# Final-norm rows and decode rows in the weight pool's slots: a hybrid decoder step on one NeuronCore

## The chip, the cores and the metric

The kernel runs on one core of a Trainium2 chip. The metric is the device time of one execution in microseconds. The core has five engines with queues of their own: PE (TensorE, matrix products), DVE (VectorE), ACT (ScalarE), POOL (GpSimd) and SP (SyncE, which here only issues DMA transfers). An engine takes its instructions strictly in the order of its queue, and an instruction that waits holds all behind it.

## The reference

One layer of a decoder trunk, for 2048 prompt rows and 8 decode rows of width 1024. Token mixing comes first (three head groups behind one input projection), then the channel mixing, and a last norm closes the trunk:

```python
mix = jnp.concatenate([y_a, y_b, y_c], axis=-1) @ w_out
x = x + gate1 * mix
hf = _rmsnorm(x, g_norm2) * (1 + scale2) + shift2
a = jax.nn.relu(hf @ w_ff1)              # hidden width 4096
x = x + gate2 * ((a * a) @ w_ff2)
...
y_prompt = _rmsnorm(xp, g_final)         # x * rsqrt(mean(x*x) + EPS) * g
y_sample = _rmsnorm(xs, g_final)
```

The change lies in the last two lines and touches nothing ahead of the product with `w_ff2`.

## The kernel before

**The second product.** `(a*a) @ w_ff2` is done in 8 passes (`NB`) over the hidden width, each with two units of 256 hidden rows (`KB = 2`). In a pass, 8 blocks follow each other, `(gi, j)` with `gi` 0 or 1 and `j` 0 to 3; a block makes two tiles of 128 rows by 1024. It uses a scheme of seven products in place of eight, each with three matmuls per unit (high and low parts), so 42 matmuls of 128x512 per block (`block`, L1805). The first four products use the first half of a block's left operands (`ai0`), the last three use the second half (`ai1`). The results lie in four PSUM banks of a block, x, y, v and z, of six there are, and DVE adds each to a sum in SBUF (`acc` for the two row tiles, `accu` for a shared term; L1396). PE can use a bank again only after DVE has drained it. In the last pass POOL and DVE then add the shared term to the row tiles.

**Operands.** The left operands of a block come by DMA from scratch memory while the block before runs (`a_load`, L1777 and L1779). For `gi = 1` one of the two units is stored unsplit, so ACT casts it (L1780) and DVE makes the low part (L1399). The right operands of a pass (tiles `wo`) are made once per pass from rows of `w_ff2` (tiles `raw2`, tag `raw` of the weight pool `wp`). Their places alternate: in every other pass, the one before the last among them, two of each unit's lie in `wp` under the tags `whi` and `wlo`; in the last pass seven of the fourteen lie in the pool `r2` under the tag `o`, and fill its 7 buffers.

**The end.** When a block of the last pass is done, its two tiles are put on a list, and `final` is called for four tiles after blocks 2, 4 and 6 and for two tiles after blocks 7 and 8. `final` squares and sums each row (ACT, L1821), multiplies half of each tile by the gain `gf` (POOL, L1832), finds the reciprocal root by a chain of small DVE operations (`row_rstd`, L188 and L119 to L124, tiles `sq`, `nr_y`, `nr_a`), scales one half on ACT (L1839) and the other on DVE (L1841), and stores each half (L1843). `samples_out` does the same for the 8 decode rows, in tiles `gs` (gate), `accs` (sum) and `xr` (residual).

**What sets the order.** The program is written by a scheduler that models each engine and puts every instruction into its engine's queue at the place where the model has it ready. A tile in a reused buffer waits for the last reader of what lay there before. SP's DMAs go through one queue; besides its data, each waits for the eighth DMA ahead of it to land.

Blocks of the last pass are called block 1 to block 8 below. Their row tiles carry these numbers in the listings: 17763 and 17765 (block 1), 17780 and 17782 (2), 17850 and 17852 (3), 17925 and 17927 (4), 17999 and 18001 (5), 18110 and 18112 (6), 18189 and 18191 (7), 18263 and 18265 (8).

Of the kernel before, what the change touches and what calls it, by code (L numbers as in the profile page):

```python
# [9 lines left out]
F32 = mybir.dt.float32  # L10
# [7 lines left out]
P = 128  # L18
D = 1024
# [30 lines left out]
R2 = 7  # L50
# [12 lines left out]
def hybrid_trunk(  # L63
# [16 lines left out]
    wp = ctx.enter_context(tc.tile_pool(name="wp", bufs=2))  # L80
# [110 lines left out]
    def load_rows(src, n, xt=None):  # L191
        if xt is None:
            xt = xpool.tile([P, D], F32, tag="x", name="xt")
        nc.sync.dma_start(out=xt[:n], in_=src)
        return xt
# [1179 lines left out]
    with ExitStack() as ph2:  # L1375
# [19 lines left out]
        def add(eng, out, in0, in1):  # L1395
            eng.tensor_tensor(out=out, in0=in0, in1=in1, op=ALU.add)  # L1396
# [268 lines left out]
        def w2_load(p, pool=None):  # L1665
            raws = []
            for i in range(2):
                raw = (pool or wp).tile([P, D], F32, tag="x" if pool else "raw", name="raw2")
                nc.sync.dma_start(out=raw, in_=w_ff2[(2 * p + i) * P:(2 * p + i + 1) * P, :])
                raws.append(raw)  # L1670
            Q.tensor_copy(out=a32[:, p % 2, :, 0:NS], in_=a_s[:, 2 * p:2 * p + 2, :])
            return raws
# [93 lines left out]
        r2 = ph2.enter_context(tc.tile_pool(name="r2", bufs=1))  # L1766
# [4 lines left out]
        def a_load(gi, j, p):  # L1771

            es = [ai.tile([P, n_, 2, P], F32R, tag=f"i{p % 2}{h}", name=f"ai{h}", bufs=2) for h, n_ in enumerate((4, 3))]
            for e, o in zip(es, (slice(0, 4), slice(4, 7))):
                e32 = e.bitcast(F32)
                if early(gi, p):
                    nc.sync.dma_start(out=e32.rearrange("p o a t -> p o (a t)"), in_=a_scr[gi][p][:, j, o])  # L1777
                else:
                    nc.sync.dma_start(out=e32[:, :, 1, :], in_=a_scr[gi][p][:, j, o])  # L1779
                    A.copy(out=e[:, :, 0, :], in_=e32[:, :, 1, :])  # L1780
                    sub(V, e[:, :, 1, :], e32[:, :, 1, :], e[:, :, 0, :])
            return es
# [3 lines left out]
        def acc_load(gi, j):  # L1786
            rows = []
            for th in range(2):
                t = 8 * gi + 4 * th + j
                r = ac.tile([P, D], F32, tag=f"r{t}", name=f"acc{t}")  # L1790
                load_rows(x1_scr[t * P:(t + 1) * P, :], P, r)
                rows.append(r)
            acc[gi, j] = rows, ac.tile([P, 512], F32, tag=f"u{gi}{j}", name=f"accu{gi}{j}")
# [29 lines left out]
        def final(tiles):  # L1823

            v = sm.tile([P, len(tiles), 2], F32, tag=f"nv{len(tiles)}", name="fv")
            if tiles[0][1] < P:
                V.memset(v, 1.0)
            for i, (x, m, _) in enumerate(tiles):
                for hf, s in enumerate(halves):
                    square_sum(x[:m, s], v[:m, i, hf:hf + 1])  # L1830
                    if hf:
                        Q.tensor_tensor(out=x[:m, s], in0=x[:m, s], in1=gf[:m, s], op=ALU.mult)  # L1832
            sq = sm.tile([P, len(tiles)], F32, tag=f"sq{len(tiles)}", name="sq")
            add(V, sq, v[:, :, 0], v[:, :, 1])
            r = row_rstd(sq, P, len(tiles), f"nr{len(tiles)}")
            for i, (x, m, dst) in enumerate(tiles):
                for hf, s in enumerate(halves):
                    if hf:
                        A.activation(out=x[:m, s], in_=x[:m, s], func=AF.Copy, scale=r[:m, i:i + 1])  # L1839
                    else:  # L1840
                        V.scalar_tensor_tensor(out=x[:m, s], in0=x[:m, s], scalar=r[:m, i:i + 1], in1=gf[:m, s],  # L1841
                                               op0=ALU.mult, op1=ALU.mult)
                    nc.sync.dma_start(out=dst[:, s], in_=x[:m, s])  # L1843

        def samples_out():
            gs, accs, xr = (r2.tile([P, D], F32, tag="o", name=n, bufs=R2) for n in ("gs", "accs", "xr"))
            nc.sync.dma_start(out=gs[0:NS].rearrange("j (k p) -> j k p", k=KT),
                              in_=g2_scr[:, 0:NS, :].rearrange("k j p -> j k p"))
            for j in range(4):
                nc.sync.dma_start(out=accs[0:NS, 256 * j:256 * j + 256], in_=chunks[32 * j:32 * j + NS])  # L1850
            load_rows(x1_scr[T:T + NS, :], NS, xr)
            Q.tensor_tensor(out=accs[:NS], in0=accs[:NS], in1=gs[:NS], op=ALU.mult)
            add(V, accs[:NS], accs[:NS], xr[:NS])
            final([(accs, NS, y_sample.rearrange("b t d -> (b t) d"))])
# [7 lines left out]
        for i, (nb, gi, j) in enumerate(steps):  # L1862
            a_now, w_now = a, w
            if i + 1 < len(steps):
                nb2, gi2, j2 = steps[i + 1]
                a = [a_load(gi2, j2, KB * nb2 + q) for q in range(KB)]
                if nb2 == 0:
                    acc_load(gi2, j2)
            if nb + 1 < NB:
                at = i % len(tiles)  # L1870
                if at == 0:
                    w_next = []
                loads, uses = ((1, 4), (3, 6)) if nb == 0 else ((1, 3), (2, 5))
                if at in loads:
                    raws = w2_load(KB * (nb + 1) + loads.index(at))
                elif at in uses:
                    w2_samples(KB * (nb + 1) + uses.index(at), raws)
                    w_next.append(w2_ops(KB * (nb + 1) + uses.index(at), raws))
                elif at == len(tiles) - 1:
                    w = w_next  # L1880
            block(nb, gi, j, w_now, a_now)
            if nb == NB - 1:
                if i == len(steps) - len(tiles):
                    gf = r2.tile([P, D], F32, tag="o", name="gf", bufs=R2)
                    nc.sync.dma_start(out=gf, in_=g_final.unsqueeze(0).to_broadcast([P, D]))
                if i == len(steps) - len(tiles) + 1:
                    samples_out()
                done += [(acc[gi, j][0][th], P, y_prompt[0, t * P:(t + 1) * P, :])
                         for th, t in enumerate((8 * gi + j, 8 * gi + 4 + j))]
                if j % 2 or gi and j == 2:  # L1890
                    final(done)
                    done = []
# [27 lines left out]
```

## Time and profile before

| | |
|---|---|
| median of 3 runs | 2496.91 us (2493.01 to 2502.81) |
| profiled execution | 2489.5 us, of which the span from first to last instruction is 2487.8 us |
| busy share of the span: PE, DVE, ACT, POOL | 94%, 76%, 44%, 28% |
| mean granted PE clock | 0.978 of full speed |

The span is what the trace shows; 1.7 us of the profiled time lie around it. All times of the trace count from the span's start. A busy share is a mean over the whole span, and stretches of it differ.

### The profile page before, as it was taken

To read this page: it belongs to the slowest core of one execution; us is meant where nothing else is said; L and a number is where in the kernel's file an instruction comes from. 1 tells how busy PE (TensorE), PEld (TensorE's weight loads), DVE (VectorE), ACT (ScalarE), POOL (GpSimd) and SP (SyncE) were. 2 spreads that over 40 slices of the span, in tenths; PEclk is the share of its full clock that TensorE was granted. 3 is DMA by queue.
4 is the path that set the end of the run, shared out by engine and by line. 5 is a ranking of instruction groups with operands and counts; after the bars stand their busy time and mean duration, and the time that the engine had idled before them with its cause. 6 is when DMAs were issued, how large, how long until landed. Compare 5 with 4: busy or idle time off the path is not lost. (4 is left out here: it accounts for less than half of the span.)

```text
span 2487.8 us, 36542 instructions
## 1 busy us (share of the span) xinstructions
PE 2340.6 (94%) x12797; PEld 1879.6 (76%) x12797; DVE 1892.3 (76%) x3378; ACT 1093.8 (44%) x2411; POOL 692.1 (28%) x469
## 2 busy tenths in 40 slices
PE   7989999999999999989999999999989999999991
PEld 3567788788999788667777767777668888888881
DVE  3986987887887586677878796767777787777767
ACT  3266247237336443455575675555532221221205
POOL 2101101011111234543237332323431223231324
PEclk9999999999999999999999999999999999999996
DMA  9976434544643567854779785656675555556553
GB/s 328 360 272 223 171 136 163 179 142 158 213 139 124 153 196 222 269 172 132 241 228 333 239 273 171 191 173 185 212 253 163 167 166 167 170 158 180 162 161 146
DMA packets 456327, 490.73 MB, mean 197 GB/s; under 512 B 40106, under 2 KB 364395, under 8 KB 456120
## 3 DMA queue, kind: packets, MB, share of 16 engines
q1 hardware_dynamic: 381296, 386.55, 48.5%
q10 hardware_dynamic: 73088, 96.48, 11.8%
q0 software_dynamic: 1760, 5.38, 0.7%
q8 instruction: 101, 1.65, 0.3%
q14 instruction: 82, 0.67, 0.1%
HBM read 335.63 MB, written 153.07 MB: 196 GB/s over the span
## 5 line engine op out<-in xcount | busy, mean ns | idle before, releaser
L180 PE MATMUL ps_ip<-hhi,whi 128*128 128x512 f32 (+1 forms) x1112 | 410.6, 370 | 11.4 <-ACT whi L151 9.2
L180 PE MATMUL ps_ip<-hhi,wlo 128*128 128x512 f32 (+1 forms) x1112 | 408.7, 368 | 8.4 <-DVE wlo L132 8.1
L180 PE MATMUL ps_ip<-hlo,whi 128*128 128x512 f32 (+1 forms) x1112 | 407.8, 367 | 4.4 <-DVE hlo L132 3.3
L180 PEld LDWEIGHTS ps_ip<-hhi,whi 128*128 128x128 f32 x1112 | 211.0, 190 | 53.2 <-ACT whi L151 10.8
L180 PEld LDWEIGHTS ps_ip<-hhi,wlo 128*128 128x128 f32 x1112 | 210.9, 190 | 48.5 <-DVE wlo L132 12.0
L180 PEld LDWEIGHTS ps_ip<-hlo,whi 128*128 128x128 f32 x1112 | 210.7, 190 | 38.7 <-DVE hlo L132 5.2
L1780 ACT CAST ai<-ai 128x512 fp32r<-128x512 f32 (+1 forms) x128 | 72.3, 567 | 350.0 <-DMA ai<-a_scr 334.4
L1805 PE MATMUL ps_v<-wo,ai 128*128 128x512 f32 x768 | 197.6, 391 | 2.4 <-DVE wo L1399 1.9
L1805 PE MATMUL ps_z<-wo,ai 128*128 128x512 f32 x768 | 197.0, 391 | 2.3 <-DVE wo L1399 1.5
L1805 PE MATMUL ps_x<-wo,ai 128*128 128x512 f32 x768 | 195.3, 395 | 1.7 <-DMA ai<-a_scr 1.7
L1571 PE MATMUL ps_v<-xo,wo 128*128 128x512 f32 x744 | 186.2, 397 | 7.3 <-DVE t L1396 5.2
L552 DVE SCALAR_TENSOR_TENSOR dc<-glu,dww,dc 128x512 f32<-128x512 f32 x240 | 189.3, 816 | 1.7
L1399 DVE TENSOR_TENSOR wo<-s,wo 128x512 fp32r<-128x512 f32 x128 | 122.5, 962 | 84.5 <-ACT wo L1402 83.4
L1571 PE MATMUL ps_x<-xo,wo 128*128 128x512 f32 x744 | 185.5, 397 | 1.0 <-ACT s L1612 0.7
L1571 PE MATMUL ps_z<-xo,wo 128*128 128x512 f32 x744 | 183.2, 394 | 0.3 <-DVE t L1396 0.3
L1402 ACT CAST wo<-raw 128x512 fp32r<-128x512 f32 x192 | 116.5, 619 | 152.3 <-POOL raw L1399 41.1
L1687 POOL TENSOR_TENSOR raw<-raw,g 128x1024 f32<-128x1024 f32 x32 | 84.2, 2653 | 353.1 <-DMA ai<-a_scr 282.6
L1399 DVE TENSOR_TENSOR ai<-ai 128x512 fp32r<-128x512 f32 (+1 forms) x128 | 100.8, 789 | 104.9 <-ACT ai L1780 104.6
L1805 PEld LDWEIGHTS ps_x<-wo,ai 128*128 128x128 f32 x768 | 145.5, 190 | 38.3 <-DVE acc L1396 3.3
L1571 PEld LDWEIGHTS ps_v<-xo,wo 128*128 128x128 f32 x744 | 137.8, 188 | 43.3 <-DVE t L1396 8.0
L1805 PEld LDWEIGHTS ps_z<-wo,ai 128*128 128x128 f32 x768 | 144.3, 188 | 33.8 <-DVE wo L1399 2.3
L1805 PEld LDWEIGHTS ps_v<-wo,ai 128*128 128x128 f32 x768 | 144.2, 188 | 33.6 <-DVE wo L1399 2.9
(507 smaller groups left out, 4774.6 us busy)
## 6 DMA issues: line engine op xcount, KB each, us to landing
a_scr<-ae SPq DMA_DIRECT2D x112, 512.0 KB
raw<-in_w_ff SPq DMA_DIRECT2D x94, 512.0 KB
whi<-w_scr ACTq DMA_DIRECT2D x66, 512.0 KB
wlo<-w_scr ACTq DMA_DIRECT2D x66, 512.0 KB
ai<-a_scr SPq DMA_DIRECT2D x64, 512.0 KB
mraw<-in_w_ada SPq DMA_DIRECT2D x48, 512.0 KB
ai<-a_scr SPq DMA_DIRECT2D x64, 384.0 KB
a_scr<-s SPq DMA_DIRECT2D x80, 256.0 KB
```

Source lines behind the costliest of these rows:

```text
L180: nc.tensor.matmul(out=ps, lhsT=a[:, k, :], rhs=b, start=(i == 0), stop=(i == 3 * KT - 1))
L552: nc.vector.scalar_tensor_tensor(out=d, in0=gt[:, j:j + GT], scalar=dww[:, t, j:j + 1], in1=d, op0=ALU.mult, op1=ALU.add)
L1399: eng.tensor_tensor(out=out, in0=in0, in1=in1, op=ALU.subtract)
L1402: A.copy(out=entry[:, 0, :], in_=full)
L1571: nc.tensor.matmul(out=ps, lhsT=w[:, a, c], rhs=x[:, b, :], start=start and i == 0, stop=stop and i == 2, skip_group_check=True)
L1687: Q.tensor_tensor(out=raw, in0=raw, in1=g2, op=ALU.mult)
L1780: A.copy(out=e[:, :, 0, :], in_=e32[:, :, 1, :])
L1805: nc.tensor.matmul(out=ps, lhsT=a[q][n // 4][:, n % 4, x, :], rhs=w[q][r][:, y, :], start=first and q == 0 and i == 0, stop=last and q == ...
```

## The change

The gain `gf`, and the three tiles of the decode rows, no longer take buffers with the tag `o` of the pool `r2`, in which the right operands of the last pass lie, but buffers of the weight pool `wp`: `gf` and `gs` under the tag `raw`, `accs` under `whi`, `xr` under `wlo`. Nothing is computed in another way.

```diff
         def samples_out():
-            gs, accs, xr = (r2.tile([P, D], F32, tag="o", name=n, bufs=R2) for n in ("gs", "accs", "xr"))
+            gs, accs, xr = (wp.tile([P, D], F32, tag=t, name=n)
+                            for t, n in (("raw", "gs"), ("whi", "accs"), ("wlo", "xr")))
...
                 if i == len(steps) - len(tiles):
-                    gf = r2.tile([P, D], F32, tag="o", name="gf", bufs=R2)
+                    gf = wp.tile([P, D], F32, tag="raw", name="gf")
                     nc.sync.dma_start(out=gf, in_=g_final.unsqueeze(0).to_broadcast([P, D]))
```

The scheduler then orders the last pass anew. The programs are the same up to this pass. In the difference listings a minus is the program before, a plus the changed one; a row is source line, operation, output and inputs with buffer numbers, and shape.

SP's queue at the end of the loads, before the change (`ai` are the left operands of block 8, `out` the results):

```order
 L1777 DMA ai_22642<-a_scr_14_11338 128x768
 L1779 DMA ai_22646<-a_scr_15_11339 128x3x128
-L1885 DMA gf<-in_g_final 128x1024
-L1847 DMA gs<-g_scr 8x8x128
-L1850 DMA accs<-chunks 8x256 x4
-L194 DMA xr<-x_scr 8x1024
-L1843 DMA out<-accs 8x512 x2
-L1843 DMA out<-acc_17763 128x512 x2
-L1843 DMA out<-acc_17765 128x512 x2
```

These rows are gone from there. The loads of `accs` and `xr` now stand ahead of the second-half operands of block 1, `gf` and `gs` around those of block 2. The stores of blocks 1 and 2 stand in the middle of the loads for block 5:

```order
 L1777 DMA ai_22333<-a_scr_14_11338 128x1024
 L1779 DMA ai_22337<-a_scr_15_11339 128x4x128
+L1843 DMA out<-acc_17763 128x512 x2
+L1843 DMA out<-acc_17765 128x512 x2
+L1843 DMA out<-acc_17780 128x512 x2
+L1843 DMA out<-acc_17782 128x512 x2
 L1777 DMA ai_22334<-a_scr_14_11338 128x768
 L1779 DMA ai_22338<-a_scr_15_11339 128x3x128
```

Eight stores have moved ahead of `ai_22334` and `ai_22338`, the second half of block 5's operands; in the same way eight more (blocks 3 and 4) now stand ahead of the loads for block 8.

DVE's queue around the first of these norms (`ps` are PSUM banks; `accu_17929` belongs to block 4, `acc_17850` and `acc_17852` to block 3):

```order
 L1396 TENSOR_TENSOR accu_17929<-ps_x,accu_17929 128x512
+L124 SCALAR_TENSOR_TENSOR nr_y<-nr_a,nr_y 128x4
+L122 TENSOR_TENSOR nr_a<-nr_y 128x4
 L1399 TENSOR_TENSOR ai_22337<-ai_22337 128x4x128
+L123 SCALAR_TENSOR_TENSOR nr_a<-nr_a,sq 128x4
+L124 SCALAR_TENSOR_TENSOR nr_y<-nr_a,nr_y 128x4
+L1841 SCALAR_TENSOR_TENSOR acc_17763<-acc_17763,nr_y,gf 128x512
+L1841 SCALAR_TENSOR_TENSOR acc_17765<-acc_17765,nr_y,gf 128x512
+L1841 SCALAR_TENSOR_TENSOR acc_17780<-acc_17780,nr_y,gf 128x512
+L1841 SCALAR_TENSOR_TENSOR acc_17782<-acc_17782,nr_y,gf 128x512
 L1396 TENSOR_TENSOR acc_17850<-ps_v,acc_17850 128x512
 L1396 TENSOR_TENSOR acc_17852<-ps_z,acc_17852 128x512
```

The rows with a plus stood behind the last drain before. Now the chain and the four scalings of blocks 1 and 2 stand between drains of blocks 3 and 4.

DVE's queue near the end of the changed program (`ps_v_22745` and `ps_z_22746` are banks of block 8, which PE uses again for its last 12 matmuls):

```order
 L1841 SCALAR_TENSOR_TENSOR acc_17999<-acc_17999,nr_y,gf 128x512
 L1841 SCALAR_TENSOR_TENSOR acc_18001<-acc_18001,nr_y,gf 128x512
 L1841 SCALAR_TENSOR_TENSOR acc_18110<-acc_18110,nr_y,gf 128x512
 L1841 SCALAR_TENSOR_TENSOR acc_18112<-acc_18112,nr_y,gf 128x512
+L1396 TENSOR_TENSOR acc_18191<-ps_z,acc_18191 128x512
+L1396 TENSOR_TENSOR acc_18265<-ps_v,acc_18265 128x512
+L1396 TENSOR_TENSOR acc_18263<-ps_x,acc_18263 128x512
+L1396 TENSOR_TENSOR acc_18265<-ps_z,acc_18265 128x512
+L1396 TENSOR_TENSOR sq<-fv 128x2
```

The scalings of blocks 5 and 6 now stand ahead of drains of block 8, where every drain stood ahead of every norm before.

## Rows read from the trace of the kernel before

**Rows 1.** The page: its first line, and its part 1 (busy time by engine).

```profile
span 2487.8 us, 36542 instructions
...
PE 2340.6 (94%) x12797; PEld 1879.6 (76%) x12797; DVE 1892.3 (76%) x3378; ACT 1093.8 (44%) x2411; POOL 692.1 (28%) x469
```

**Rows 2.** Windows: busy us (instructions) of PE, PEld, DVE, ACT, POOL; clock, DMA.

```profile
2361.00:2438.00 77.00, 76.27 (x337) 62.84 (x336) 50.27 (x74) 7.40 (x15) 24.22 (x18) 1.00 0.45 138
...
2438.00:2488.00 50.00, 0.59 (x3) 0.16 (x1) 38.44 (x92) 33.56 (x81) 21.56 (x17) 0.53 0.45 169
```

**Rows 3.** Timeline of SP's DMA queue in the last pass: start, us, what.

```profile
2385.92 0.37 SPq L1779 DMA_DIRECT2D ai<-a_scr  x1
...
2391.81 0.32 SPq L1777 DMA_DIRECT2D ai<-a_scr  x1
...
2426.04 0.33 SPq L1885 DMA_DIRECT2D gf<-in_g_final  x1
...
2430.80 0.29 SPq L194 DMA_DIRECT2D xr<-x_scr  x1
```

**Rows 4.** Timeline of ACT, second half of the last pass: start, us, what [idle before].

```profile
2389.88 0.62 ACT L1780 CAST ai<-ai 128x512 fp32r<-128x512 f32 x1 [25.27 <-DMA ai<-a_scr]
...
2395.70 0.52 ACT L1780 CAST ai<-ai 128x384 fp32r<-128x384 f32 x1 [5.19 <-DMA ai<-a_scr]
```

**Rows 5.** Chain that ended last, two places one block apart.

```profile
2395.41 2.72 PE ps_x L1805 x12
...
2404.93 2.72 PE ps_x L1805 x12
```

**Rows 6.** Timeline of PE, the last matmuls.

```profile
2436.94 1.65 PE L1805 MATMUL ps_z<-wo,ai 128*128 128x512 f32 x6 [0.73 <-DVE acc L1396]
```

**Rows 7.** Groups by line after the matmuls: count, busy us, mean ns, idle before.

```profile
L1832 POOL TENSOR_TENSOR acc<-acc,gf 128x512 f32<-128x512 f32 x16 | 20.3, 1271 | 18.5 <-ACT junk L1821 18.1 <-DVE nr_a L123 0.2
...
L1821 ACT ACTIVATE junk<-acc 128x512 bf16<-128x512 f32 x32 | 20.1, 628 | 0.9
...
L1841 DVE SCALAR_TENSOR_TENSOR acc<-acc,nr_y,gf 128x512 f32<-128x512 f32 x16 | 11.1, 748 | 0.1
```

**Rows 8.** Timeline of DVE after the matmuls.

```profile
2433.98 2.30 DVE L1396 TENSOR_TENSOR accs<-accs,xr 8x1024 f32<-8x1024 f32 x1 [1.13 <-POOL accs L1852]
...
2445.76 0.16 DVE L1396 TENSOR_TENSOR sq<-fv 128x4 f32<-128x4 f32 x1 [0.70 <-ACT junk L1821]
...
2447.34 1.27 DVE L122 TENSOR_TENSOR nr_a<-nr_y 128x4 f32<-128x4 f32 x1
...
2448.64 0.16 DVE L123 SCALAR_TENSOR_TENSOR nr_a<-nr_a,sq 128x4 f32<-128x4 f32 x1
...
2451.32 2.74 DVE L1841 SCALAR_TENSOR_TENSOR acc<-acc,nr_y,gf 128x512 f32<-128x512 f32 x4
...
2482.00 1.42 DVE L1841 SCALAR_TENSOR_TENSOR acc<-acc,nr_y,gf 128x512 f32<-128x512 f32 x2
```

**Rows 9.** Timeline of POOL, same stretch.

```profile
2447.32 1.27 POOL L1832 TENSOR_TENSOR acc<-acc,gf 128x512 f32<-128x512 f32 x1 [0.24 <-ACT junk L1821]
```

**Rows 10.** Timeline of DVE, start of the last pass.

```profile
2366.89 0.69 DVE L1396 TENSOR_TENSOR acc<-ps_z,acc 128x512 f32<-128x512 f32 x1 [0.46 <-PE ps_z L1805]
...
2367.61 1.17 DVE L1396 TENSOR_TENSOR acc<-acc,accu 128x512 f32<-128x512 f32 x1
```

**Rows 11.** Timeline of SP's DMA queue, the last four stores.

```profile
2482.81 1.80 SPq L1843 DMA_DIRECT2D out<-acc  x4
```

**Rows 12.** Windows after the matmuls, as in Rows 2 (last column GB/s).

```profile
2452.00:2456.00 4.00, 0.00 (x0) 0.00 (x0) 2.06 (x4) 3.94 (x10) 1.27 (x1) 0.50 0.78 289
...
2464.00:2468.00 4.00, 0.00 (x0) 0.00 (x0) 1.87 (x5) 3.84 (x12) 2.57 (x3) 0.50 1.01 378
```

**Rows 13.** Windows at the end of the matmuls, as in Rows 2.

```profile
2438.00:2440.00 2.00, 0.59 (x3) 0.16 (x1) 1.97 (x5) 1.94 (x6) 1.85 (x2) 1.00 0.00 0
...
2441.00:2442.00 1.00, 0.00 (x0) 0.00 (x0) 0.99 (x1) 0.97 (x3) 1.00 (x1) 0.50 0.00 0
```

## The prediction

> **What bounds the kernel now.** The page comes first: PE is busy 94% of the span and nothing else comes near [rows 1], so a change that saves time must either shorten PE's work or the stretch in which PE has none. The windows view, cut at the last pass, shows that second stretch. In the 77 us before 2438 PE works without a gap to speak of; in the 50 us behind it PE does 0.59 us, while DVE and ACT are busy 38.4 and 33.6 us [rows 2]. The last six matmuls start at 2436.94 and take 1.65 us [rows 6], so PE is done at 2438.6 and the span runs 2487.8 − 2438.6 = **49.2 us** longer.
>
> What is done there is the final norm of all 16 row tiles and of the decode rows [rows 7]. Why so late? Seven of the eight blocks are finished before 2438. The timeline of SP's queue gives the reason: the load of `gf` is issued at 2426.04, behind the last operand load, and that of `xr` at 2430.80 [rows 3]. They lie in buffers of the last pass's operands and must wait until PE has read these for the last time. The sum of the decode rows comes at 2433.98 [rows 8], and every norm stands behind it in DVE's and ACT's queues.
>
> **What the change removes.** This wait. `gf` and `gs` take the places of `w_ff2` rows that were read for the last time when the last pass's operands were made, `accs` and `xr` those of operands of the pass before. All four are free by the first block of the last pass, and their loads stand there in the new order. No instruction is added: the same squares, chains, scalings and stores are done, earlier. Nothing waits for `gf` ahead of PE's first block: its load stands in SP's queue among loads for block 2, which are needed a block, 9.52 us, later (two places of the chain one block apart, 2404.93 − 2395.41 [rows 5]).
>
> **What stays behind the last matmul.** Only the last pair of tiles (block 8), with the remainder of block 7. From rows: the last drain 0.7 us [rows 10]; two squares at 0.63, with their read-outs some 0.8 each, 1.6; the rest of block 7's chain, 7 operations at 0.2 (0.16 and the gap behind it), 1.4, and its two scalings, 1.42; block 8's own chain, 12 operations, 2.4, and two scalings, 1.42 [rows 7, 8]; then from the last DVE operation (2482.00 + 1.42 = 2483.42) to the end of the span 4.4 us for the stores [rows 8, 11]. Sum 0.7 + 1.6 + 1.4 + 1.4 + 2.4 + 1.4 + 4.4 = **13.3 us**. The gap of 49.2 shrinks by 35.9, if PE ends when it did.
>
> **What it costs PE.** It won't. DVE drains PSUM, and its queue is served in order. In the last pass it was busy 50.3 of 77 us, and 38.4 us of work stood behind PE's end [rows 2], 88.7 in all. Of these, 0.7 + 1.4 + 1.4 + 2.4 + 1.4 = 7.3 us stay behind the last matmul (the DVE terms above). The other 81.4 us must now be done before DVE can drain the banks that PE's last 12 matmuls use, since the order puts the scalings of blocks 5 and 6 ahead of these drains. From 2361 to 2438.6 there are 77.6 us: 3.8 too few. Also, in the first block, 9.5 us, there is nothing yet to norm, and DVE idles there by its share, 26.7 of 77, so 3.3 us are lost. That makes 7.1 us. Against it stands that some of the long chain operations (next paragraph) get shorter, and for it that DVE will stand now and then before a tile that hasn't landed; I let these cancel and take **7 us**, PE's end near 2446. The bounds are nothing, where PE hides all because a block leaves DVE 26.7 / 8 = 3.3 us, and 15, worked out under the range.
>
> **POOL's share.** In the tail a norm of four tiles takes DVE 2451.32 + 2.74 − 2445.76 = 8.3 us. Its chain, 12 small operations, takes 5.56 of these where 12 x 0.2 would be 2.4: 3.2 us more. The trace shows where: one of them takes 1.27 us where its neighbour takes 0.16, and it starts at 2447.34, just when POOL starts its own 1.27 us multiplication at 2447.32 [rows 8, 9]. Some 1.07 us each, that is three long ones per group, and the 38.4 us hold them. A PSUM drain takes 0.69, but the addition of two SBUF tiles behind it takes 1.17 [rows 10], so I take drains to be free of it. If each of the 13 multiplications that move ahead of PE's end costs DVE its whole length, it is 13 x 1.27 = 16.5 us against the 3 x 3.2 = 9.6 counted in three groups, 6.9 us more; I keep the rows' three per group and leave the 6.9 to the range.
>
> The Trainium skill, "SBUF — State Buffer", section "Who interferes with whom", states that a DVE instruction with two SBUF inputs is blocked for a whole GpSimd instruction that reads SBUF, while one with at most one such input, outside the two-port modes, is not. It speaks against a change that puts POOL's multiplications beside a DVE that is now the one waited for; read in its hardest way it gives the 6.9 us, 2475 in place of 2468, and the long and short operations above agree with it in kind.
>
> **SP's queue.** Eight stores of finished tiles now stand ahead of operand loads, twice. Before, the first half of block 5's operands was issued at 2385.92 and its cast started at 2389.88, 4 us later [rows 3, 4]; with cast and subtraction it is ready at 2391.2, and PE reads it from 2395.41 + 1.36 + 0.68 = 2397.5 [rows 5]: 6.3 us in hand. The second half was issued at 2391.81, cast at 2395.70, ready at 2396.9, and read from 2404.93 + 0.68 = 2405.6: 8.7 in hand. Block 2's second half begins two blocks ahead of block 4's 2395.41, at 2376.4, and with 12 matmuls of block 3 among its 18 ends 30 x 0.227 = 6.8 us later, at 2383.2 (0.227 is 9.52 / 42). Its norm can begin one drain later; its 8.3 us and some five drains at 0.69 between bring the scalings to about 2395. Eight stores are issued at some 0.5 us each [rows 11], and the loads behind them at about 2398, 6 us late for the second half. Landing, they follow 2 MB of stores, which drain at 289 to 378 GB/s [rows 12], in 5.5 to 7 us from 2393 on, and so hardly overtake the issue. 6 of 8.7 us: hidden, by 2 to 3 us. If the stores are that much later, or in the way for longer, PE waits some 2 us per group, 4 in all; in the range, not in the sum.
>
> **The sum.** −35.9 + 7 = **−29 us**. The profiled execution of 2489.5 would become about 2460.5. It is 7.4 us below the median of the runs shown, 2496.91, and all of them lie above it, so for the time I take the median less 29: **2468 us**.
>
> **Rivals.** First, *nothing of the norm is hidden by PE* (chance 0.08): each moved DVE operation delays a drain, and PE by as much. Three groups of 8.3 us ahead of the last matmul are 25 us, so PE ends at 2463.6, and 49.2 − 13.3 − 25 leaves a gain of 11: 2486. DVE's 26.7 idle us speak against it; that these idles are short ones between drains, and two groups fall together with casts' subtractions, speaks for it.
>
> Second, *the norm stays behind PE* (0.04): one of the four tiles still waits for something of the last pass, and the order of DVE's queue only moves its wait. The time is then 2497. Against it is that the places' last readers are in the pass before or its first block.
>
> Third, and on the other side, *the stores hold back the loads* (0.05). A load behind the eight stores waits for them to be issued, and for the eighth DMA ahead, a store, to land. If PE stood through a whole group, from its scalings to the landing of the next operands (8 x 0.5 issue, up to 7 landing, 4 for the loads, 1.3 cast and subtraction, 16.3 us) less the 6.3 in hand, that is 10 us, and twice 20: 2488. To be slower by over 0.5% each would have to cost PE 29 / 2 + 12.5 / 2 = 21 us; only a norm held up by 11 us more on DVE, since DVE itself waits for a late operand's cast, gives that. Then 2512.
>
> Fourth, *PE isn't delayed* (0.07): 2461.
>
> My forecast has the rest, 0.76, with a range of its own from 2460 to 2480.
>
> **Range and chances.** About 0.5%, 12.5 us, is what a measurement of this kernel can tell from no change. Below, the gain is at most 35.9 us, so 2461, and the runs spread some 4 us below the median: 2457. Above, three bounds add up: 6.9 us for POOL, 4 for the loads, and a fall of the clock. After PE's last matmul the granted clock stood at 1.00 until 2440 and at 0.50, 1.2 in place of 2.4 GHz, from 2441 [rows 13]. If a pause of PE ahead of the last 18 matmuls brings that, they take 18 x 0.227 = 4.1 us more. 2468 + 15 = 2483. Range 2457 to 2483. Faster by over 0.5%, below 2484.4: the forecast, the fourth rival and 0.03 of the first, 0.86; within 0.5%: the rest of the first, the second and a fifth of the third, 0.10; slower: the rest of the third, 0.04.
>
> **What would show each step.** In the changed profile `gf` should be issued near 2359 to 2367, and stores should start near 2393, not 2452. PE's end should lie near 2446, with the idle time ahead of its last `ps_v` and `ps_z` matmuls released by DVE's L1396; the span should run 13 us beyond it. DVE should be busy over 90% from 2372 on. Long waits of PE for DMA `ai`, or of DVE for ACT's casts, would show the third rival; DVE's small operations of over 1 us in more than three places per group that POOL costs more than the rows say. The forecast is wrong if PE ends after 2455, or if the chain behind it is longer than 20 us.

## The result, and the profile after

The changed kernel takes **2471.62 us** (median of 4 runs, 2471.12 to 2472.63), the kernel before 2495.49 (median of 4 beside them, 2493.01 to 2502.81): a ratio of 0.9901, interval 0.9886 to 0.9916. The forecast was 2468, range 2457 to 2483, and faster.

The first line and part 1 of the page of the changed kernel, which answer to [rows 1]:

```profile
span 2469.4 us, 36558 instructions
...
PE 2351.1 (95%) x12797; PEld 1884.0 (76%) x12797; DVE 1887.8 (76%) x3378; ACT 1092.2 (44%) x2411; POOL 694.3 (28%) x469
```

The windows that answer to [rows 2], same columns:

```profile
2361.00:2438.00 77.00, 73.22 (x319) 59.30 (x318) 67.06 (x118) 30.11 (x71) 37.83 (x27) 1.00 0.65 214
2438.00:2488.00 50.00, 14.51 (x52) 10.93 (x50) 24.03 (x57) 12.36 (x29) 8.90 (x7) 0.82 0.24 89
```

Each engine has as many instructions as before; DVE's and ACT's work has moved from the second window into the first. These clocks can't be laid over each other, though: the profiled run of the changed kernel reached the last pass some 7 us later than that of before, by work that the change doesn't touch. From here on times are counted from the start of PE's twelve x matmuls at the **border of the last pass's first and second block**, which each trace shows: six are block 1's last, six block 2's first. (Some expectations call this point PE's first matmul of the second block; that one comes 1.36 us later.) Timeline of PE, the kernel before:

```profile
2366.69 2.88 PE L1805 MATMUL ps_x<-wo,ai 128*128 128x512 f32 x12
```

and the changed kernel, with its pauses and its last matmuls:

```profile
2373.86 2.88 PE L1805 MATMUL ps_x<-wo,ai 128*128 128x512 f32 x12
...
2404.75 1.65 PE L1805 MATMUL ps_x<-wo,ai 128*128 128x512 f32 x6 [0.81 <-DVE acc L1396]
...
2427.71 1.64 PE L1805 MATMUL ps_y<-wo,ai 128*128 128x512 f32 x6 [2.80 <-DVE acc L1396]
...
2445.51 1.52 PE L1805 MATMUL ps_x<-wo,ai 128*128 128x512 f32 x6
2451.10 2.92 PE L1805 MATMUL ps_v<-wo,ai 128*128 128x512 f32 x6 [4.07 <-DVE acc L1396]
2453.83 2.76 PE L1805 MATMUL ps_z<-wo,ai 128*128 128x512 f32 x6
```

Before, PE ended 2438.59 − 2366.69 = 71.9 us after that point [rows 6], with a tail of 49.2 us: 121.1 in all. After, it ends at 2453.83 + 2.76 = 2456.59, 82.7 us after it, with a tail of 2469.4 − 2456.6 = 12.8: 95.5 in all. The pass gains 25.6 us: the tail gives 36.4, PE's delay of 10.8 takes part of it back. The medians differ by 23.9; the profiled run of before lay 6 us under its median, that of after on it, so the two spans alone show only 18.4.

Of the 10.8 us, 7.1 are pauses: 7.8 where the kernel before had one of 0.73 [rows 6]. The view of PE's waits names one line for all of them:

```profile
PE ps_v L1805 <- DVE acc L1396: 4.1, 1, 4.1
PE ps_y L1805 <- DVE acc L1396: 2.8, 1, 2.8
PE ps_x L1805 <- DVE acc L1396: 1.0, 2, 0.8
```

Another 2.5 us are in the last twelve matmuls, and 1.2 in no single place. The last twelve run from 2451.10 to 2456.59, 5.49 us, where before six usually stood 1.36 us from the next six and the last six took 1.65. The granted clock in the windows there, behind POOL's busy time, stands at 0.50, 1.2 in place of 2.4 GHz:

```profile
2451.00:2453.00 2.00, 1.90 (x5) 1.51 (x6) 2.00 (x4) 1.71 (x6) 0.90 (x1) 0.50 1.03 381
2453.00:2455.00 2.00, 2.00 (x6) 1.61 (x5) 1.92 (x6) 0.08 (x1) 0.40 (x1) 0.50 0.64 241
```

What DVE did ahead of the two long pauses, its timeline (the drains at 2426.98 and 2450.36 are the ones PE stood for, near 2427.7 and 2451.1):

```profile
2423.30 3.75 DVE L1841 SCALAR_TENSOR_TENSOR acc<-acc,nr_y,gf 128x512 f32<-128x512 f32 x4
2426.98 0.68 DVE L1396 TENSOR_TENSOR acc<-ps_z,acc 128x512 f32<-128x512 f32 x1
...
2443.17 0.82 DVE L122 TENSOR_TENSOR nr_a<-nr_y 128x4 f32<-128x4 f32 x1
2444.03 1.21 DVE L123 SCALAR_TENSOR_TENSOR nr_a<-nr_a,sq 128x4 f32<-128x4 f32 x1
2445.27 1.21 DVE L124 SCALAR_TENSOR_TENSOR nr_y<-nr_a,nr_y 128x4 f32<-128x4 f32 x1
...
2447.11 2.74 DVE L1841 SCALAR_TENSOR_TENSOR acc<-acc,nr_y,gf 128x512 f32<-128x512 f32 x4
2449.76 0.68 DVE L1396 TENSOR_TENSOR acc<-ps_z,acc 128x512 f32<-128x512 f32 x1
2450.36 0.68 DVE L1396 TENSOR_TENSOR acc<-ps_v,acc 128x512 f32<-128x512 f32 x1
```

Each time four scalings of a norm stand ahead of the drains, and ahead of the second four also a chain with operations of 0.8 to 1.2 us where 0.16 is usual. POOL's timeline beside that chain has a multiplication (L1832) and then two additions of the shared term (L1396), so two of the three long operations stand beside additions, which the kernel before has as well:

```profile
2442.68 1.29 POOL L1832 TENSOR_TENSOR acc<-acc,gf 128x512 f32<-128x512 f32 x1 [2.44 <-ACT junk L1821]
2443.93 2.53 POOL L1396 TENSOR_TENSOR acc<-acc,accu 128x512 f32<-128x512 f32 x2
```

The queue of SP, which answers to [rows 3, 11], with `gf` loaded early, the stores in four lots, and loads between them:

```profile
2365.95 0.33 SPq L1886 DMA_DIRECT2D gf<-in_g_final  x1
...
2389.87 0.70 SPq L1843 DMA_DIRECT2D out<-accs  x2
...
2402.17 4.47 SPq L1843 DMA_DIRECT2D out<-acc  x8
2406.72 0.60 SPq L1777 DMA_DIRECT2D ai<-a_scr  x1
2407.42 0.60 SPq L1779 DMA_DIRECT2D ai<-a_scr  x1
...
2424.08 4.46 SPq L1843 DMA_DIRECT2D out<-acc  x8
...
2447.92 18.32 SPq L1843 DMA_DIRECT2D out<-acc  x16
```

One wait is longer than it should be. The loads of block 5's second half (384 and 192 KB) are issued at 2406.72 and 2407.42, right behind the eight stores and, with the 7.2 us between the traces taken off, 7.7 us later than before (2391.81 [rows 3]). ACT casts it at 2412.70, 9.8 us later than before (2395.70 [rows 4]), and DVE stands for that:

```profile
2413.24 0.77 DVE L1399 TENSOR_TENSOR ai<-ai 128x384 fp32r<-128x384 f32 x1 [3.15 <-ACT ai L1780]
```

PE's matmuls wait for no DMA and no cast in this pass; its weight loads wait once, 0.4 us, for a cast. But PE's own order is no longer that of before, which neither the listings of the change nor the prediction have. From block 5 on, where left operands are cast, the scheduler mixes the matmuls of neighbouring blocks, in runs of nine, three and two where the order before had twelve x at a border. Timeline of PE, the changed kernel:

```profile
2413.06 2.23 PE L1805 MATMUL ps_x<-wo,ai 128*128 128x512 f32 x9
2415.13 0.85 PE L1805 MATMUL ps_y<-wo,ai 128*128 128x512 f32 x3
```

What this order costs or saves by itself, no run shows.

### The profile page after: what moved, and what is told of

Read it like the earlier page. It is cut to its first block, busy times and chain, and to the rows that moved or that the text cites. A ratio compares the mean times of both kernels' runs of the same rounds, so it can differ in the third digit from the quotient of the medians.

```text
span 2469.4 us, 36558 instructions
## 1 busy us (share of the span) xinstructions
PE 2351.1 (95%) x12797; PEld 1884.0 (76%) x12797; DVE 1887.8 (76%) x3378; ACT 1092.2 (44%) x2411; POOL 694.3 (28%) x469
## 3 DMA queue, kind: packets, MB, share of 16 engines
q8 instruction: 101, 1.65, 0.3%
## 5 line engine op out<-in xcount | busy, mean ns | idle before, releaser
L180 PEld LDWEIGHTS ps_ip<-hhi,wlo 128*128 128x128 f32 x1112 | 212.4, 191 | 47.7 <-DVE wlo L132 10.8
L1399 DVE TENSOR_TENSOR ai<-ai 128x512 fp32r<-128x512 f32 (+1 forms) x128 | 107.2, 840 | 101.8 <-ACT ai L1780 101.0
```

The lines of the kernel that those rows point to most:

```text
L180: nc.tensor.matmul(out=ps, lhsT=a[:, k, :], rhs=b, start=(i == 0), stop=(i == 3 * KT - 1))
L1399: eng.tensor_tensor(out=out, in0=in0, in1=in1, op=ALU.subtract)
```

## The experiments

Three theories stood for PE's delay, and none excludes the others. *Theory 1*: DVE's own norm work, and its place in DVE's order ahead of the drains. *Theory 2*: POOL's multiplications lengthen DVE's operations. *Theory 3*: the stores, in SP's queue and on the way to memory, make operands late. (The expectation of no_early_stores calls the stores theory 2, that of scale_act calls POOL theory 3.) The table has every run, counted as above; some expectations count from the pass's start, which is 9.52 − 1.36 = 8.16 us earlier, so 8.2 is to be added to the second column for them (before 80.1, after 90.9).

| run | PE's end | tail | sum | ratio to before (interval) |
|---|---|---|---|---|
| before | 71.9 | 49.2 | 121.1 | 1 |
| after | 82.7 | 12.8 | 95.5 | 0.9901 (0.9886 to 0.9916) |
| gf_only | 71.3 | 49.4 | 120.6 | 0.9996 (0.9985 to 1.0008) |
| decode_only | 80.6 | 27.5 | 108.1 | 0.9942 (0.9919 to 0.9965) |
| no_early_stores | 77.8 | 13.4 | 91.2 | 0.9894 (0.9869 to 0.9920) |
| scale_act | 85.6 | 16.3 | 101.9 | 0.9903 (0.9885 to 0.9922) |
| no_pool_mult | 77.6 | 11.7 | 89.2 | 0.9858 (0.9842 to 0.9875) |
| no_dve_scale | 77.1 | 14.0 | 91.1 | 0.9877 (0.9859 to 0.9894) |
| late_group | 77.5 | 18.1 | 95.6 | 0.9889 (0.9871 to 0.9907) |
| dve_both | 74.3 | 18.7 | 92.9 | 0.9875 (0.9860 to 0.9890) |
| act_stores | 80.1 | 13.3 | 93.5 | 0.9888 (0.9872 to 0.9904) |
| mix_two | 77.8 | 17.4 | 95.3 | 0.9894 (0.9875 to 0.9914) |
| mix_three | 75.6 | 20.0 | 95.6 | 0.9894 (0.9881 to 0.9908) |
| dve_two_queues | 74.3 | 18.6 | 92.9 | 0.9896 (0.9880 to 0.9913) |

That border lay between 2365.3 and 2373.9 us in these profiles, for work that is the same in all. So the times can't order kernels that differ by 3 us; the columns from the traces, one profiled run each, can better (two kernels that differ only in a queue, dve_both and dve_two_queues, agree within 0.1 us). The ratios are to the kernel before as it ran beside each: its median was 2495.5 us beside the changed kernel and 2491.8 to 2493.4 beside the others, so the changed kernel's ratio is, if anything, flattered by some 0.1%.

The scheduler orders every run anew, so a run can change more than its edit. In the last pass no_pool_mult has every queue in the changed kernel's order, and late_group has PE's. gf_only has PE's order of before. In the other runs PE's and DVE's orders differ as well (the last three runs have PE's order of dve_both), and what they show is edit and order together.

**The two halves of the change.** gf_only moves `gf` alone:

```diff
-            gs, accs, xr = (wp.tile([P, D], F32, tag=t, name=n)
-                            for t, n in (("raw", "gs"), ("whi", "accs"), ("wlo", "xr")))
+            gs, accs, xr = (r2.tile([P, D], F32, tag="o", name=n, bufs=R2) for n in ("gs", "accs", "xr"))
```

> Only the gain moves to the weight pool; the three tiles of the decode rows stay among the last pass's operands. If it is enough that the gain is early, the time is that of the changed kernel, about 2472 us. If the sum of the decode rows, which stands ahead of all norms in the queues of ACT and DVE, is what holds them, nothing moves: about 2495 us, with the stores again starting 13 us or more behind the last matmul.

No gain at all. decode_only moves the other three and leaves `gf` late:

```diff
-                    gf = wp.tile([P, D], F32, tag="raw", name="gf")
+                    gf = r2.tile([P, D], F32, tag="o", name="gf", bufs=R2)
```

> Only the decode rows' tiles move; the gain is loaded late, as before. Squares and chains can then run under the matmuls, scalings and stores cannot. Behind the last matmul stand POOL's 17 multiplications of 1.27 us, one after the other, 21.6 us, and some 7 us of loading and storing: a tail of about 29 us where it was 49 before and is 13 with both moved. With half of the drains' delay (5 us) the time is about 2495 - 20 + 5 = 2480 us. If the gain alone were the point, 2495 us.

The time is as expected, 2480.5 us, its parts less so: a tail of 27.5 us for 29, and PE's end 8.7 us later for 5. The squares and part of the norm come earlier, the multiplications by `gf` don't; DVE stands 2.0 us for `gf` with drains behind it, then does scalings ahead of them, and PE's longest pause is 5.8 us. So `gf` alone gives nothing and the decode rows alone 13.0 of the 25.6 us: the whole takes both, as the prediction's account of two waits in one queue has it.

**The stores.** no_early_stores leaves out the 16 stores of the row tiles of blocks 1 to 4:

```diff
-                    nc.sync.dma_start(out=dst[:, s], in_=x[:m, s])
+                    if dst is not None:
+                        nc.sync.dma_start(out=dst[:, s], in_=x[:m, s])
...
-                done += [(acc[gi, j][0][th], P, y_prompt[0, t * P:(t + 1) * P, :])
+                done += [(acc[gi, j][0][th], P, y_prompt[0, t * P:(t + 1) * P, :] if gi else None)
```

> Leaves out the 16 stores of the first four blocks, which stand ahead of operand loads in SP's queue; their norm is computed as before. Theory 1, DVE's queue is what delays PE (norm operations ahead of PSUM drains): the pauses of PE in blocks 7 and 8 stay, since the scalings of blocks 3 to 6 stand where they stood; DVE's one wait of 3.2 us for a late operand goes. 2467 to 2471 us. Theory 2, the stores hold back the loads: most of PE's 11 us go, 2461 to 2463 us.

PE ends 4.9 us sooner, and the time, 2465.1 us, lies between the two ranges expected. The pause of 2.80 us in block 7 is gone, the last one stays at 3.39, and DVE's waits for casts fall from 3.3 to 0.2 us. act_stores keeps every store and only issues them from ACT:

```diff
-                    nc.sync.dma_start(out=dst[:, s], in_=x[:m, s])
+                    nc.scalar.dma_start(out=dst[:, s], in_=x[:m, s])
```

> A whole kernel: the norm's stores are issued from ACT's queue in place of SP's, so that no operand load stands behind a store in SP's queue; they still land at the same time. Theory 3 (SP's queue holds block 5's second half back): DVE's wait of 3.1 us for ACT's cast of it goes, and with it the pause of 2.80 us in block 7, PE ends 78 to 79 us after the start of the last pass's second block in place of 82.7, as without the stores (77.8). Rival a (it is the landing of 2 MB that delays the loads): the wait and the pause stay, PE at 82 to 83. Rival b (ACT waits for a scaling at its stores, with casts behind them): DVE's waits for ACT grow, PE at 84 or later.

DVE's waits for casts, in the view of DVE's waits of that run:

```profile
DVE ai L1399 <- ACT ai L1780: 0.9, 1, 0.9
```

So it was the order in SP's queue more than the landing that made that cast late. But PE gains only 2.6 of the 4.9 us: a pause of 1.78 us in block 7 stays of the 2.80, and 4.27 us before the last v. The first step of theory 3, late loads that DVE stands for, is shown. Its price is not: PE's and DVE's orders differ in both runs, and what goes with the stores themselves wasn't taken apart.

**POOL.** scale_act takes the scalings from DVE, and pays with 17 more multiplications on POOL and 17 more scalings on ACT:

```diff
-                    if hf:
-                        Q.tensor_tensor(out=x[:m, s], in0=x[:m, s], in1=gf[:m, s], op=ALU.mult)
+                    Q.tensor_tensor(out=x[:m, s], in0=x[:m, s], in1=gf[:m, s], op=ALU.mult)
...
-                    if hf:
-                        A.activation(out=x[:m, s], in_=x[:m, s], func=AF.Copy, scale=r[:m, i:i + 1])
-                    else:
-                        V.scalar_tensor_tensor(out=x[:m, s], in0=x[:m, s], scalar=r[:m, i:i + 1], in1=gf[:m, s],
-                                               op0=ALU.mult, op1=ALU.mult)
+                    A.activation(out=x[:m, s], in_=x[:m, s], func=AF.Copy, scale=r[:m, i:i + 1])
```

> Both halves of a tile are multiplied by the gain on POOL and scaled on ACT, so DVE loses its 17 scalings of 0.68 us (11.6 us, 8.8 of them ahead of PE's end), POOL gets 17 multiplications more and ACT 17 scalings. Theory 1, DVE's queue: PE's delay shrinks by most of 8.8 us and the clock does not fall before the end (2.8 us): 2460 to 2464 us. Theory 3, POOL's multiplications hold up DVE: twice as many of them, so no gain or a loss, 2470 to 2478 us.

PE ends 2.9 us *later*, although 13 operations of 0.68 us, 8.8 in all, are gone from DVE ahead of PE's end; the time, 2468.3 us, lies between the two ranges expected. Its timeline of DVE has one reason, behind which PE pauses 2.14 us:

```profile
2374.17 6.16 DVE L123 SCALAR_TENSOR_TENSOR nr_a<-nr_a,sq 128x1 f32<-128x1 f32 x1
2380.25 0.68 DVE L1396 TENSOR_TENSOR acc<-ps_v,acc 128x512 f32<-128x512 f32 x1
```

and its timeline of POOL beside it:

```profile
2374.07 2.53 POOL L1831 TENSOR_TENSOR accs<-accs,gf 8x512 f32<-8x512 f32 x2
2376.57 4.96 POOL L1831 TENSOR_TENSOR acc<-acc,gf 128x512 f32<-128x512 f32 x4
```

An operation on one column, 0.16 us long elsewhere, takes 6.16 us while POOL works through five multiplications in a row. Up to PE's end DVE has 16 instructions less and is busy 73.3 us, where it was 73.9. That isn't all of the loss: DVE waits 7.8 us for casts on ACT in place of 3.3, and PE once 1.6 us for a load. no_pool_mult leaves out POOL's multiplications, and with them the factor `gf` in the second halves:

```diff
-                    if hf:
-                        Q.tensor_tensor(out=x[:m, s], in0=x[:m, s], in1=gf[:m, s], op=ALU.mult)
```

> Leaves out POOL's 17 multiplications by gf of the second halves of rows, so the output lacks that factor there; DVE's and ACT's scalings, the stores and the order stay. In the changed kernel PE's last matmul ends 90.9 us after the last pass's start, with 7.8 us of pauses (2.80 and 4.07 the longest), all released by DVE. Theory 2 (POOL's multiplications hold DVE's operations on two SBUF inputs): about 10 us of lengthened operations go from DVE, the pause of 4.07 us and the clock's fall behind it with them; PE ends 82 to 85 us after the start, and the small operations over 1 us that stay lie beside POOL's additions of acc and accu. Theory 1 (it is DVE's own scalings that stand ahead of the drains, 2.74 and 3.75 us in a row): both pauses stay, PE ends at 88 to 91. Theory 3 (the stores): 90.

Windows from that border to PE's end, the changed kernel:

```profile
2373.86:2456.59 82.73, 74.88 (x313) 59.59 (x311) 73.87 (x134) 35.24 (x85) 43.69 (x33) 0.96 0.57 189
```

and this run:

```profile
2366.58:2444.14 77.56, 73.07 (x313) 59.36 (x311) 63.88 (x134) 35.17 (x85) 22.27 (x17) 0.98 0.61 202
```

POOL has 16 instructions and 21.4 us less, and DVE with the **same 134 instructions** is busy 10.0 us less. That is the price of POOL's multiplications on DVE, 0.62 us each; no queue's order has changed with the edit. PE ends 5.1 us sooner. But the last pause stays, behind the same four scalings:

```profile
2439.53 2.78 PE L1805 MATMUL ps_v<-wo,ai 128*128 128x512 f32 x6 [3.33 <-DVE acc L1396]
```

So the expected 82 to 85 (theory 2) was not quite reached, 85.7, and the order (theory 1) has its own part. So have POOL's *additions*: in this run two operations of the chain ahead of that pause are still long. DVE's timeline, and the line of POOL's beside it:

```profile
2432.38 1.28 DVE L123 SCALAR_TENSOR_TENSOR nr_a<-nr_a,sq 128x4 f32<-128x4 f32 x1
2433.70 1.22 DVE L124 SCALAR_TENSOR_TENSOR nr_y<-nr_a,nr_y 128x4 f32<-128x4 f32 x1
...
2432.36 2.54 POOL L1396 TENSOR_TENSOR acc<-acc,accu 128x512 f32<-128x512 f32 x2 [7.70 <-DVE nr_a L122]
```

They take 2.2 us more than at the usual 0.16 each.

**DVE's own work.** no_dve_scale leaves out DVE's scalings, so first halves are stored as they are:

```diff
-                    else:
-                        V.scalar_tensor_tensor(out=x[:m, s], in0=x[:m, s], scalar=r[:m, i:i + 1], in1=gf[:m, s],
-                                               op0=ALU.mult, op1=ALU.mult)
```

> Leaves out DVE's 17 scalings of the first halves of rows, which are stored as they are; POOL's multiplications, ACT's scalings and all stores stay. Theory 1 (DVE's own scalings ahead of the drains): 13 x 0.68 = 9 us go from DVE before PE's end, both long pauses and the clock's fall go, PE ends 81 to 84 us after the last pass's start (90.9 in the changed kernel). Theory 2 (POOL's holds): the long small operations stay, the pause before the last v falls from 4.07 only by the 2.74 us of scalings, to some 1.3, and PE ends at 85 to 87. Theory 3 (the stores hold back loads): a pause in block 7 stays, PE at 88.

PE's end at 85.3 from the start is in theory 2's range, but not by its reason alone: the last pause falls to 0.70, and one of 2.5 us comes before a z, with DVE waiting 10.9 us for casts in all. late_group keeps everything and calls the norm of blocks 5 and 6 behind block 7:

```diff
-                if j % 2 or gi and j == 2:
+                if j == 3 or j == (2 if gi else 1):
```

> A whole kernel: the norm of blocks 5 and 6 is called behind block 7 with its two tiles, as one group of six, so that DVE has none of its operations ahead of the drains for PE's last v and z. Theory 1 (what stands ahead of these drains makes the last pause): the pause of 4.07 us and the clock's fall behind it go, PE ends 83 to 85 us after the last pass's start in place of 90.9, while four more tiles of scalings and eight more stores make the tail 16 to 17 us in place of 12.8: 3 us faster than the changed kernel. Rival (POOL's additions of acc and accu hold DVE there, whatever the norm does): a pause of over 2 us stays, PE at 88, and the time is as in the changed kernel or 2 us longer.

The last matmuls of that run have no pause ahead of them and no slow clock:

```profile
2444.74 1.52 PE L1805 MATMUL ps_z<-wo,ai 128*128 128x512 f32 x6
```

The last pause and the fall of the clock behind it go together, and PE, in the same order as in the changed kernel, ends 5.2 us sooner (85.7 from the start, for 83 to 85): the place of these four tiles' norm makes both. It would be more, but the pause of 2.80 us in block 7 stays, and here the granted clock stands at 0.50 behind it, from 2424.6 to 2426.0. But the tail grows by 5.3, all of it, where 3 to 4 had been expected. The sum, 95.6, is the changed kernel's, 95.5: the wait has only changed sides.

**DVE alone.** dve_both takes POOL and ACT out of the scaling; DVE does both halves, 17 operations of 0.68 us more:

```diff
-                    if hf:
-                        Q.tensor_tensor(out=x[:m, s], in0=x[:m, s], in1=gf[:m, s], op=ALU.mult)
...
-                    if hf:
-                        A.activation(out=x[:m, s], in_=x[:m, s], func=AF.Copy, scale=r[:m, i:i + 1])
-                    else:
-                        V.scalar_tensor_tensor(...)
+                    V.scalar_tensor_tensor(out=x[:m, s], in0=x[:m, s], scalar=r[:m, i:i + 1], in1=gf[:m, s],
+                                           op0=ALU.mult, op1=ALU.mult)
```

> A whole kernel: both halves of a row are scaled and multiplied by gf in DVE's one operation, POOL's 17 multiplications and ACT's 17 scalings go. DVE has 13 x 0.68 = 9 us more of its own work ahead of PE's end. Theory 2 (each of POOL's multiplications costs DVE nearly its length, some 10 us in all): the two cancel, PE ends 88 to 92 us after the last pass's start (90.9 in the changed kernel), the time is within 3 us of the changed kernel. Theory 1 (DVE's own work alone counts): the pauses grow from 7.8 to some 16 us, PE ends at 98 or later, the time is 5 to 8 us longer.

Better than either theory had it: PE ends 8.4 us sooner than in the changed kernel. One part is theory 2. Another is that the scheduler now puts the third group's scalings behind the drains for PE's last matmuls, as DVE's timeline shows:

```profile
2438.38 0.69 DVE L1396 TENSOR_TENSOR acc<-ps_z,acc 128x512 f32<-128x512 f32 x1
...
2439.45 0.68 DVE L1396 TENSOR_TENSOR acc<-ps_z,acc 128x512 f32<-128x512 f32 x1
...
2440.84 4.06 DVE L1836 SCALAR_TENSOR_TENSOR acc<-acc,nr_y,gf 128x512 f32<-128x512 f32 x6
```

so they lengthen the tail, to 18.7. How much each part gives, and how much PE's changed order, isn't shown. The sum is 2.6 us below the changed kernel's. The two ratios' intervals overlap, so a gain over the changed kernel is seen in the pass and not shown in the time.

**Three versions on top of it.** mix_two and mix_three keep DVE alone for the first groups and share the last ones with POOL and ACT:

```diff
-        def final(tiles):
+        def final(tiles, late=False):
-                    if hf:
+                    if hf and late:      # both places
...
-                    final(done)
+                    final(done, gi == 1)               # mix_two: blocks 5 to 8 shared
+                    final(done, gi == 1 and j > 1)     # mix_three: blocks 7 and 8 shared
```

> A whole kernel: the norms of blocks 1 to 4 and of the decode rows are scaled and multiplied by gf on DVE alone, those of blocks 5 to 8 are shared with POOL and ACT as in the changed kernel. Counted from PE's first matmul of the last pass's second block: in the changed kernel PE ends after 82.7 us with a tail of 12.8, with DVE alone for all groups after 74.3 with a tail of 18.7. Theory 2 (POOL's multiplications beside PE's blocks cost DVE some 10 us): with 9 of them gone and the third group's scalings behind the last drains, PE ends at 75 to 77, and the shared last groups shorten the tail to 13 to 15; the sum 89 to 91, 4 to 6 us below the changed kernel. Rival (what DVE alone gained lies in the order of its scalings, not in POOL): PE ends at 79 or later.

> A whole kernel: as the one before, but blocks 5 and 6 too on DVE alone; only blocks 7 and 8 are shared with POOL and ACT. Theory 2: PE ends at 74 to 75 us after the start of the last pass's second block, as with DVE alone (74.3), the tail loses four of DVE's sixteen scalings, 2.7 us, and is 16; the sum 90 to 91. Rival (a shared tail gains nothing, since POOL holds DVE's chain of block 8 there): 92 to 93 as with DVE alone.

Both missed: sums of 95.3 and 95.6, worse than with DVE alone. In mix_three the chains of blocks 7 and 8 have again operations of 1.25, 1.28 and 1.11 us, each beside a multiplication of POOL; these 3.2 us are more than the four scalings saved, 2.7. The rival was right that a shared tail gains nothing there; its 92 to 93 was missed too, by 2.6 us, of which these operations explain some 0.5. dve_two_queues is dve_both with the second halves' stores issued from ACT's queue:

```diff
-                    nc.sync.dma_start(out=dst[:, s], in_=x[:m, s])
+                    (nc.scalar if hf else nc.sync).dma_start(out=dst[:, s], in_=x[:m, s])
```

> A whole kernel: all scalings with gf on DVE alone, as in the run of that kind (PE's end 74.3 us after its first matmul of the last pass's second block, tail 18.7, sum 92.9), and the stores of second halves issued from ACT's queue, those of first halves from SP's. In the tail of that run SP issues its last 16 stores in 16.2 us, about one per us. Theory (SP's queue and DVE's scalings share the bound there): the stores keep up with the scalings, the tail is 17 to 18, PE's end as it was, the sum 91 to 92. Rival (ACT's casts of block 7's and 8's operands now stand behind stores that wait for DVE's scalings): PE ends at 76 or later, and the sum is 93 to 95.

Nothing moved, neither PE's end nor the tail. The tail with DVE alone is DVE's, not the queue's: the last eight of its scalings and two chains stand one behind the other.

## Why the prediction was right, point by point

**What was removed, and the tail.** Right, and in its size: 12.8 us for 13.3, and the last DVE operation stands 2463.64 + 1.42 = 2465.06, 4.3 us ahead of the end, for 4.4. `gf` is issued at 2365.95, in before's time 7.2 us less, 2358.8, for 2359 to 2367; the first eight stores at 2402.17, so 2395.0, for 2393.

**What it costs PE.** The mechanism is as written, DVE's queue with scalings ahead of drains: every pause is released by L1396, and from 2379 to 2451 DVE is busy 65.9 of 72 us, 92%. The term was too small, 7 for 10.8, and its parts were further off than their sum. The window that the prediction counted from 2361 to PE's end, in the changed kernel, with the same 338 matmuls:

```profile
2368.17:2456.59 88.42, 80.57 (x338) 64.28 (x336) 77.70 (x140) 36.49 (x87) 45.07 (x33) 0.96 0.57 190
```

DVE is busy for 77.7 us there, not 81.4: 0.1 too much for the 77.6 us, in place of 3.8. It is idle for 10.7 us, not 3.3. So the two things that the prediction let cancel did not: DVE's operations got 3.7 us shorter, and it stood 7.4 us longer, 7.1 − 3.7 + 7.4 = 10.8. Of the idle time 3.3 us are waits for casts, some 2.8 fall into the first 9.8 us, 1.0 are waits for the squares of the first norms, and some 1.5 are DVE's wait for PE's last, slowed matmuls. That 7 came as near as it did is in part luck. The clock's fall behind the last pause, 2.5 us, is a part of the 10.8; the prediction had worked it out as 4.1 and left it in the range, since it took a pause ahead of the last 18 matmuls for a possibility.

**POOL's share.** The 9.6 us for POOL held in size: 10.0 measured with DVE's instructions unchanged. That it would be three long operations per group, all by multiplications, did not: the first group has three, of which two stand beside POOL's additions, the third has four, of which two do, and the second group has its loss in the scalings (3.75 us for four, 2.74 elsewhere) and in a subtraction. The Trainium skill, "SBUF — State Buffer", section "Who interferes with whom", has DVE operations with at most one SBUF input, outside the two-port modes, free of the lock that DVE and GpSimd share, and operations with two SBUF inputs held by it (a drain, with one of its inputs in PSUM, is of the first kind). The trace agrees: in scale_act a drain takes 0.68 us beside POOL's sixth multiplication, and the operation in front of it 6.16 beside the first five. The page has the lock last for one instruction; here DVE's wait lasted for five.

**SP's queue.** That it would be hidden was wrong. The second half's loads were issued 7.7 us late, for 6, and its cast came 9.8 us late, for 8.7 in hand. PE's matmuls wait for no load all the same, but in an order that the prediction didn't have. The delay comes out as 3.15 us in which DVE stands for the cast, with its queue already full, and, as no_early_stores and act_stores make likely, through it in a part of PE's pause in block 7. That step looked only at when PE needs the operand, and DVE makes it ready. Issuing the stores from another queue gave 2.6 us back, leaving 16 out 4.9, each with an order of its own.

**The rivals.** Nothing hidden, the norm behind PE, and stores that cost more than the gain did not come: a tail of 12.8 us and PE's end 10.8 later exclude all three. That PE isn't delayed was wrong too.

**The base.** That the profiled run of before lay under its median was met by taking the median less the gain. The error of the time is then 10.8 − 7 = 3.8 for PE, −0.5 for the tail, and −1.4 since the median beside the changed runs was 2495.5 and not 2496.9, which leaves 1.7 us that the traces don't have: 3.6 in all.

**Left open.** Leaving out the stores, POOL's multiplications or DVE's scalings, or calling one group later, gives 4.9, 5.1, 5.6 and 5.2 us, 20.8 together, of a delay of 10.8. So the causes overlap. Two of these are shown without a change of PE's order, POOL's multiplications and the late group. How the 2.80 us pause divides, and what PE's order has to do with it, no run here says.

## What to carry to other kernels

When work is moved under a busy engine, add up what the engine that serves it must now do before its last release, with its lengthened operations, add the time in which it will itself stand for something, and look at the place in its order: here its work just fitted, and 10.7 us of idle time of its own are what PE's delay amounts to, with the longest pause near the end and a fall of the clock behind it. Taking work from a full engine and giving it to one that holds it up can be a loss: DVE with 32 scalings of its own came out 2.6 us better in the pass than DVE with 16 and POOL beside it. A scheduler that orders everything anew can move the waiting engine's own instructions too, so its order belongs in the comparison. And an operand's slack is counted to the first engine in the chain that must handle it, not to the one that reads it last.

## What the runs showed of the hardware

An operation of DVE with two SBUF inputs was held for 6.16 us while POOL ran five instructions back to back, not only for the one under way. POOL can be held in the same way: in decode_only a multiplication of 8x512 that starts at 2434.88, 0.11 us after the first of DVE's seven scalings in a row, takes 6.34 us, where 1.27 is usual. Operations with one SBUF input are held as well, as DVE's timeline of the changed kernel has it (L188 and L119, usually 0.17), while POOL adds for 2.53 us from 2393.20 and multiplies for 1.29 from 2395.69:

```profile
2394.54 1.22 DVE L188 TENSOR_SCALAR sq<-sq 128x4 f32<-128x4 f32 x1
2395.79 1.21 DVE L119 TENSOR_SCALAR nr_y<-sq 128x4 int32<-128x4 int32 x1
```

After a pause of 4.07 us the granted clock stood at 0.50, and six matmuls took 2.92 us; after one of 2.80 the next six took 1.64 in the changed kernel and 2.02 in late_group, and after one of 2.45 in no_dve_scale 2.38.
